# Attention on one core: the order of transposes, copies and small jobs inside a step

## Chip, core and metric

The kernel runs on one core of one Trainium2 chip. The metric is the device time of one execution in microseconds (us), told as the median of several runs. Before the change the median of three runs was 1228.65 us (1227.79 to 1230.59).

## What is computed

The reference is a trunk of two layers on a sequence of 512 tokens with 1024 channels. Layer 0 mixes tokens with a convolution module, layer 1 with a sparse attention; a gated feed-forward stage follows each. The change lies in the attention. With 8 blocks of 64 tokens and 16 blocks to choose from at most, every valid block is selected, and the window of 512 covers the sequence, so both the "selected" and the "window" branch are causal attention over all 512 keys, with keys and values of their own. A third branch attends to 31 compressed blocks. The core of it:

```
def chunk(c):
    ...
    p_c = masked_softmax(s_c, cmp_end[None, :] <= t[:, None])
    o_c = jnp.einsum('bgrqn,bgnd->bgrqd', p_c, v_cmp)
    ...
    p_s = masked_softmax(s_s, tok <= t[:, None])
    o_s = jnp.einsum('bgrqk,bgqkd->bgrqd', p_s, v_s)
    ...
    p_w = masked_softmax(s_w, mask_w)
    o_w = jnp.einsum('bgrqk,bgkd->bgrqd', p_w, vw)
    ...
    return g[0] * o_c + g[1] * o_s + g[2] * o_w
```

There are 16 query heads of 64 channels in 4 groups, and the three outputs are added with a gate for each head and token.

## The kernel before, in words

The whole trunk is one program. The stages follow each other: convolution, first feed-forward, projections of the attention, the loop over heads, the output projection, second feed-forward. Matrix products of the large stages are done in parts: a rounded value and a remainder ("h" and "l" tiles), with three products for one.

The change lies in the loop over heads (the `for n in range(1, N + 2)` at L1861). Its unit of work is a pair of heads, `j` from 0 to 7, and a branch, `br` 1 (selected) or 2 (window), which makes N = 16 units; unit n holds two heads, called `par` 0 and 1 ("head 0" and "head 1" here). A step n does three things at once:

- Scores of unit n: `sc_` calls `score` (L1750) for each of the four query tiles t = 3, 2, 1, 0 of a head. TensorE makes the product S in PSUM (L1760 and L1761, 128 x 128(t+1), at least 256 wide), VectorE (DVE) adds the mask, writes `Pm` to SBUF and takes the extreme value `mx` (L1763), ScalarE (ACT) takes the exponential and its sum `sm` (L1764). Three PSUM banks hold S in turn.
- `weigh_` (L1768): DVE takes the reciprocal of two sums (L1774), and GpSimd (POOL) scales the two tiles by it and by the gate (L1778).
- Unit n - 1, scored and weighed in the step before: `flip_` (L1781) transposes 128 x 128 blocks of `Pm` on TensorE (L1791) into a PSUM bank, four at a time, and one engine copies the bank to SBUF: tag `t1` by DVE (L1794), tags `t0` and `t2` by ACT (L1796). A pair such as (0, 2) means head 0, key block 2; key block kc has 4 - kc transposes, since the mask is causal. So `t2` holds key block 2 of both heads, a `t1` key blocks 1 and 3 of one head, a `t0` key block 0 of one head. `values` (L1800) multiplies them with v (L1817) and adds up in a bank `O`; blocks 3, 2 and 1 at the end of step n, block 0 early in step n + 1.

The transposes, the compressed scores `psc` and the transposed compressed weights `pct` share three PSUM banks (tag "p2"). `O` has two banks of its own.

The compressed branch of a pair of heads is prepared by `q_pair` (L1478). It gives small jobs to named slots "a", "b", "c", "d" of certain steps: `move` (DMAs on the SP queue, L1490), `stack_hi` (L1493, ACT or POOL) and `stack_lo` (L1504, DVE), `scores` (L1509, TensorE, into `psc`), `masked`, `top`, `minus`, `sums` (DVE), `exps` (ACT), `valid` and `weighed` (POOL), `trans` (L1554, four transposes into `pct`) and `parts` (L1560: a rounded copy `pch` by ACT, the remainder `pcl` by DVE). For p = 1, 2, 3 `trans` runs in step 4p, for p = 0 in step 1; `scores` runs in steps 1, 2, 4, 5, 8 and 9. In odd steps `values` begins a new `O` with three products of `pch` and `pcl` (L1809 to L1811). When a head pair is done, in odd steps from 3 on, `o_hi` (ACT, L1828) and `o_lo` (DVE, L1834) copy it out. At the end of steps 14 and 16 a weight of the output projection is split (`w_hi` on ACT, L219; `w_lo` on DVE, L228).

Inside the loop every engine keeps the order in which the program issues its instructions (`tc.keep_in_program_order`); an instruction that waits holds those behind it on its engine. So the order of the calls at L1884 to L1914 is the order of all queues.

Of the kernel before, what the change touches and what calls it, by code (L numbers as in the profile page):

```python
# [120 lines left out]
def trunk(ctx: ExitStack, tc: tile.TileContext, A, out):  # L121
    nc = tc.nc
# [8 lines left out]
    def nm(s):  # L131
        cnt[0] += 1
        return f"{s}_{cnt[0]}"
# [1065 lines left out]
    def nsa(acc, gnext):  # L1199
# [275 lines left out]
        def kept(z):  # L1475
            return tc.keep_in_program_order(z) if fixed[0] else z

        def q_pair(p):  # L1478
# [78 lines left out]
                    tc.keep_in_program_order(nc.tensor.transpose(  # L1557
                        pt[:, t * P:(t + 1) * P], sc[:, t].rearrange("p j n -> p (j n)"), ident))

            def parts():  # L1560
                pt = box["pct"]
                ph = q3[1].tile([P, T], F32R, tag="pch", name=nm("pch"))
                pl = q3[1].tile([P, T], F32R, tag="pcl", name=nm("pcl"))
                kept(nc.scalar.activation(ph, pt, AF.Copy))
                kept(nc.vector.tensor_tensor(pl, pt, ph, ALU.subtract))
                pcT[p] = (ph, pl)

            def both(jj):
# [4 lines left out]
            if p == 0:  # L1573
                return [lambda: (move(0), scores(0), masked(0)), lambda: (both(0), scores(1), masked(1)),
                        lambda: (move(1), top(), minus(), exps()), lambda: (both(1), valid(), sums(), weighed()),
                        trans, parts]
            n = 4 * p - 4
            jobs = {
                (n, "c"): [lambda: scores(0)],
# [19 lines left out]
            }  # L1599
            jobs.update({  # L1600
                (n + 4, "a"): [trans, lambda: stack_hi(1)],
                (n + 4, "c"): [parts],
                (n + 4, "d"): [lambda: stack_lo(1, 0)],
                (n + 5, "a"): [lambda: stack_lo(1, 1)],
            })
# [194 lines left out]
        def values(Us, kcs):  # L1800


            j, br = Us[0]["j"], Us[0]["br"]
            a = j // 4
            if br == 1 and kcs[0] == 3:
                ob[j] = (p2, pO)[j % 2].tile([P, T], F32, tag="O", name=nm("O"), bufs=1)
                ph, pl = pcT[j // 2]
                ch, cl = vcb[a, j % 2]
                pe(nc.tensor.matmul(ob[j], ch, ph, start=True, stop=False))  # L1809
                pe(nc.tensor.matmul(ob[j], ch, pl, start=False, stop=False))  # L1810
                pe(nc.tensor.matmul(ob[j], cl, ph, start=False, stop=False))  # L1811
            o = ob[j]
            for kc in kcs:
                last = br == 2 and kc == 0
                for par in range(2):
                    g = slice((2 * a + par) * DH, (2 * a + par + 1) * DH)
                    pe(nc.tensor.matmul(o[par * 64:par * 64 + 64, P * kc:], vf[br][:, kc, g], Us[par][kc], start=False,  # L1817
                                        stop=last))
                if last:
                    split_o.append(j)  # L1820
# [40 lines left out]
        for n in range(1, N + 2):  # L1861
            S = n < N
            F = n <= N
            if S:
                start(n)

            def sc_(par, *ts):
                if S:
                    for t in ts:
                        score(U[n][par], t)  # L1870

            def weigh_(par, t):
                if S:
                    weigh(U[n][par], t)

            def flip_(tag, eng, *parts):
                if F:
                    flip([(U[n - 1][par], t) for par, t in parts], tag, eng)

            def slot(z):  # L1880
                for f in work.pop((n, z), ()):
                    f()

            sc_(0, 3, 2)  # L1884
            flip_("t2", nc.scalar, (0, 2), (1, 2))
            if n > 1:
                values(U.pop(n - 2), (0,))
            if n == 1:
                qp0[4]()
            slot("a")  # L1890
            weigh_(0, 2)
            sc_(0, 1, 0)
            slot("b")
            o_hi()
            flip_("t1", nc.vector, (0, 1), (0, 3))
            sc_(1, 3)
            weigh_(0, 0)
            flip_("t1", nc.vector, (1, 1), (1, 3))
            sc_(1, 2)
            o_lo()  # L1900
            if n == 1:
                qp0[5]()
            slot("c")
            flip_("t0", nc.scalar, (0, 0))
            sc_(1, 1, 0)
            weigh_(1, 2)
            flip_("t0", nc.scalar, (1, 0))
            slot("d")
            weigh_(1, 0)
            if n in W_AT:  # L1910
                w_hi(state["next"] + W_AT.index(n))
                w_lo(state["next"] + W_AT.index(n))
            if F:
                values(U[n - 1], (3, 2, 1))  # L1914
        assert not work, work
        fixed[0] = hold[0] = False
        sx.close()
# [180 lines left out]
```

## Time and profile before

| what | value |
|---|---|
| median of three runs | 1228.65 us (1227.79 to 1230.59) |
| the profiled execution's own time | 1228.15 us |
| its span, first to last instruction | 1226.3 us |
| PE (TensorE matmul) busy | 1195.1 us, 97% of the span |
| DVE busy | 901.8 us, 74% |
| ACT busy | 603.5 us, 49% |
| POOL busy | 244.4 us, 20% |
| mean granted TensorE clock | 0.997 |
| the attention loop, steps 1 to 16 | from 687.35 to 832.74 us of the span |

PE is the matmul side of TensorE, PEld its weight load, SP the engine that issues most DMAs. A busy PE means that matmuls are under way, not that they run at their peak. A row of the timeline reads: start in us, duration, engine, line, operation, output and inputs with their shapes, how many instructions are merged into the row, and in brackets how long the engine stood idle before it and what released it. The chain of waits is followed back from an end to whatever released each instruction. Names lose their numbers: `T` is the bank of a transpose, `t` its copy in SBUF, `S` a score, `O` an output.

### The profile page before, as it was taken

To read this page: it belongs to the slowest core of one execution; us is meant where nothing else is said; L and a number is where in the kernel's file an instruction comes from. 1 tells how busy PE (TensorE), PEld (TensorE's weight loads), DVE (VectorE), ACT (ScalarE), POOL (GpSimd) and SP (SyncE) were. 2 spreads that over 40 slices of the span, in tenths; PEclk is the share of its full clock that TensorE was granted. 3 is DMA by queue.
4 is the path that set the end of the run, shared out by engine and by line. 5 is a ranking of instruction groups with operands and counts; after the bars stand their busy time and mean duration, and the time that the engine had idled before them with its cause. 6 is when DMAs were issued, how large, how long until landed. Compare 5 with 4: busy or idle time off the path is not lost.

```text
span 1226.3 us, 22079 instructions
## 1 busy us (share of the span) xinstructions
PE 1195.1 (97%) x8519; PEld 1039.0 (85%) x8519; DVE 901.8 (74%) x1722; ACT 603.5 (49%) x1116; POOL 244.4 (20%) x349
## 2 busy tenths in 40 slices
PE   9999999999999999999998899989999999999998
PEld 6788778799999989987677766657878999998998
DVE  6996598877777576865688778764597777776675
ACT  5221464455555444544344677773354555554443
POOL 2021002011111102211333466651000111110120
PEclk9999999999999999999999999999999999999999
DMA  8748628267777667554156011006323877765882
GB/s 308 269 129 300 174 86 240 86 176 184 184 185 179 151 193 162 122 169 112 59 129 175 28 27 32 13 18 172 115 91 110 198 185 182 190 165 123 227 166 91
DMA packets 88378, 181.11 MB, mean 148 GB/s; under 512 B 36816, under 2 KB 38480, under 8 KB 86736
## 3 DMA queue, kind: packets, MB, share of 16 engines
q1 hardware_dynamic: 66816, 109.99, 29.6%
q0 software_dynamic: 21456, 69.71, 25.0%
q8 instruction: 67, 1.10, 0.4%
q14 instruction: 39, 0.32, 0.1%
HBM read 165.60 MB, written 5.80 MB: 140 GB/s over the span
## 4 chain that ended last, share of the span: by engine, by line
PE 80%; DVE 9%; issue 3%; ACT 3%; DMA 2%; SPq 2%; POOL 1%; DVEq 0%; POOLq 0%; ACTq 0%
PE st L915 28%; PE st L1105 10%; PE pp L281 7%; PE pp L279 7%; PE pp L280 7%; PE st L281 2%; PE st L280 2%; PE st L279 2%; PE cpe L540 2%; PE O L1817 2%; PE T L1791 2%; PE pv L1653 2%; DVE wl L228 1%; PE S L1760 1%; DVE Pm L1763 1%
## 5 line engine op out<-in xcount | busy, mean ns | idle before, releaser
L219 ACT ACTIVATE wh<-wr 128x1024 fp32r<-128x1024 f32 (+4 forms) x150 | 152.8, 1019 | 196.0 <-PE pp L280 63.0
L228 DVE TENSOR_TENSOR wl<-wr,wh 128x1024 fp32r<-128x1024 f32 (+4 forms) x150 | 181.4, 1209 | 47.2 <-ACT wh L219 46.8
L915 PE MATMUL st<-bh,sl 128*128 128x256 f32 x680 | 192.6, 283 | 1.1 <-DVE sl L899 1.1
L915 PE MATMUL st<-bh,sh 128*128 128x256 f32 x680 | 192.7, 283 | 0.0
L915 PE MATMUL st<-bl,sh 128*128 128x256 f32 x680 | 192.0, 282 | 0.0
L281 PE MATMUL pp<-hh,wl 128*128 128x512 f32 x400 | 158.1, 398 | 3.9 <-DVE wl L228 3.9
L279 PE MATMUL pp<-hh,wh 128*128 128x512 f32 x400 | 159.6, 401 | 2.2 <-ACT wh L219 2.1
L280 PE MATMUL pp<-hl,wh 128*128 128x512 f32 x400 | 158.7, 398 | 0.1
L915 PEld LDWEIGHTS st<-bh,sl 128*128 128x128 f32 x680 | 130.2, 192 | 1.5 <-DVE sl L899 1.5
L915 PEld LDWEIGHTS st<-bl,sh 128*128 128x128 f32 x680 | 130.6, 192 | 0.1
L915 PEld LDWEIGHTS st<-bh,sh 128*128 128x128 f32 x680 | 130.0, 191 | 0.1
L899 DVE TENSOR_TENSOR sl<-S,sh 128x512 fp32r<-128x512 f32 x136 | 87.9, 688 | 51.9 <-ACT sh L898 51.9
L279 PEld LDWEIGHTS pp<-hh,wh 128*128 128x128 f32 x400 | 75.4, 189 | 23.4 <-ACT wh L219 4.5
L281 PEld LDWEIGHTS pp<-hh,wl 128*128 128x128 f32 x400 | 75.5, 189 | 23.2 <-DVE wl L228 5.9
L1778 POOL TENSOR_SCALAR Pm<-Pm,sm,gates 128x512 f32<-128x512 f32 (+3 forms) x128 | 81.0, 643 | 62.5 <-DVE sm L1774 59.0
L280 PEld LDWEIGHTS pp<-hl,wh 128*128 128x128 f32 x400 | 75.7, 189 | 18.6 <-issue 1.1
L1764 ACT ACTIVATE Pm<-Pm,mx 128x512 f32<-128x512 f32 (+3 forms) x128 | 71.0, 556 | 39.9 <-DVE mx L1763 35.4
L1105 PE MATMUL st<-oz,soh 128*128 128x256 f32 x448 | 79.7, 280 | 0.0
L898 ACT ACTIVATE sh<-S 128x512 fp32r<-128x512 f32 x136 | 77.5, 619 | 0.0
L915 PE MATMUL st<-bl,wh 128*128 128x256 f32 x272 | 76.2, 280 | 0.0
L915 PE MATMUL st<-bh,wh 128*128 128x256 f32 x272 | 76.1, 280 | 0.0
L915 PE MATMUL st<-bh,wl 128*128 128x256 f32 x272 | 76.1, 280 | 0.0
(308 smaller groups left out, 2770.1 us busy)
## 6 DMA issues: line engine op xcount, KB each, us to landing
S<-fw_x POOLq DMA_DIRECT2D x68, 512.0 KB, 5.9
wr<-fw_in SPq DMA_DIRECT2D x46, 512.0 KB
So<-fw_q POOLq DMA_DIRECT2D x38, 448.0 KB, 6.4
bd<-bands POOLq DMA_DIRECT2D x12, 1280.0 KB, 12.4
wr<-fw_q SPq DMA_DIRECT2D x24, 448.0 KB
r<-fw_x SPq DMA_DIRECT2D x34, 256.0 KB
wr<-fw_p SPq DMA_DIRECT2D x16, 512.0 KB
wr<-cw_in SPq DMA_DIRECT2D x14, 512.0 KB
```

Source lines behind the costliest of these rows:

```text
L219: parted(after(nc.scalar.activation(hi[:, :cols], raws[i][:, :cols], AF.Copy), pin.get(AF)))
L228: parted(after(nc.vector.tensor_tensor(lo[:, :cols], raws[i][:, :cols], hi[:, :cols], ALU.subtract), pin.get(ALU)))
L279: held(nc.tensor.matmul(ps, wh, xh, start=first, stop=False))
L280: held(nc.tensor.matmul(ps, wh, xl, start=False, stop=False))
L281: held(nc.tensor.matmul(ps, wl, xh, start=False, stop=last))
L540: last["conv"] = nc.tensor.matmul(ps[e * 64:e * 64 + 16 * m, g, :], w, f[:, g0 + g, 4 - s:68 - s], start=s == 0, stop=s == 4)
L898: pe(nc.scalar.activation(h_[:, c], z, AF.Copy))
L899: pe(nc.vector.tensor_tensor(l_[:, c], z, h_[:, c], ALU.subtract))
L915: pe(nc.tensor.matmul(ps[:, :H], p_[:, k], m_[c][:, t], start=first and c == 0 and q == 0, stop=last and c == 3 and q == 2, skip_group_che ...
L1105: pe(nc.tensor.matmul(ps, a[:, c], b[:, t], start=p in (1, 4) and i == 0 and r == 0, stop=i == NO - 1 and r == 2, skip_group_check=True))
L1764: kept(nc.scalar.activation(Pt, Pt, AF.Exp, bias=mx, scale=-1.0, accum_out=sm))
L1778: kept(nc.gpsimd.tensor_scalar(Pt, Pt, sm[:, k:k + 1], gates[:, t + k, br * 16 + h:br * 16 + h + 1], ALU.mult, ALU.mult))
```

## The change

The transposes and copies of a step come in another order. Before, the order was `t2` of both heads (ACT), `t1` of head 0 (DVE), `t1` of head 1 (DVE), `t0` of head 0 (ACT), `t0` of head 1 (ACT). After, it is `t1` of head 0, `t0` of head 0, `t2` of both heads, `t1` of head 1, `t0` of head 1, on the same engines. `o_hi` moves from behind slot b to behind slot a, `o_lo` from behind the score (1, 2) to ahead of it. The job `parts` is split: `part_hi` (ACT) goes to slot b and `part_lo` (DVE) to slot c, where both were. Slot b now stands behind the `t0` of head 0. In step 1 the jobs of p = 0 go through the slots a, b and c too. The products of `values` at the end of a step take key blocks 2, 3, 1 in place of 3, 2, 1. No instruction is added or taken away.

```
--- before.py
+++ after.py
@@ -1557,12 +1557,15 @@
                     tc.keep_in_program_order(nc.tensor.transpose(
                         pt[:, t * P:(t + 1) * P], sc[:, t].rearrange("p j n -> p (j n)"), ident))
 
-            def parts():
-                pt = box["pct"]
+            def part_hi():
                 ph = q3[1].tile([P, T], F32R, tag="pch", name=nm("pch"))
+                kept(nc.scalar.activation(ph, box["pct"], AF.Copy))
+                pcT[p] = (ph,)
+
+            def part_lo():
+                ph, = pcT[p]
                 pl = q3[1].tile([P, T], F32R, tag="pcl", name=nm("pcl"))
-                kept(nc.scalar.activation(ph, pt, AF.Copy))
-                kept(nc.vector.tensor_tensor(pl, pt, ph, ALU.subtract))
+                kept(nc.vector.tensor_tensor(pl, box["pct"], ph, ALU.subtract))
                 pcT[p] = (ph, pl)
 
             def both(jj):
@@ -1573,7 +1576,7 @@
             if p == 0:
                 return [lambda: (move(0), scores(0), masked(0)), lambda: (both(0), scores(1), masked(1)),
                         lambda: (move(1), top(), minus(), exps()), lambda: (both(1), valid(), sums(), weighed()),
-                        trans, parts]
+                        trans, part_hi, part_lo]
             n = 4 * p - 4
             jobs = {
                 (n, "c"): [lambda: scores(0)],
@@ -1599,7 +1602,8 @@
             }
             jobs.update({
                 (n + 4, "a"): [trans, lambda: stack_hi(1)],
-                (n + 4, "c"): [parts],
+                (n + 4, "b"): [part_hi],
+                (n + 4, "c"): [part_lo],
                 (n + 4, "d"): [lambda: stack_lo(1, 0)],
                 (n + 5, "a"): [lambda: stack_lo(1, 1)],
             })
@@ -1802,7 +1806,7 @@
 
             j, br = Us[0]["j"], Us[0]["br"]
             a = j // 4
-            if br == 1 and kcs[0] == 3:
+            if br == 1 and 3 in kcs:
                 ob[j] = (p2, pO)[j % 2].tile([P, T], F32, tag="O", name=nm("O"), bufs=1)
                 ph, pl = pcT[j // 2]
                 ch, cl = vcb[a, j % 2]
@@ -1881,27 +1885,26 @@
                 for f in work.pop((n, z), ()):
                     f()
 
+            if n == 1:
+                for z, f in zip("abc", qp0[4:]):
+                    work.setdefault((n, z), []).insert(0, f)
             sc_(0, 3, 2)
-            flip_("t2", nc.scalar, (0, 2), (1, 2))
+            flip_("t1", nc.vector, (0, 1), (0, 3))
             if n > 1:
                 values(U.pop(n - 2), (0,))
-            if n == 1:
-                qp0[4]()
             slot("a")
+            o_hi()
             weigh_(0, 2)
             sc_(0, 1, 0)
+            flip_("t0", nc.scalar, (0, 0))
             slot("b")
-            o_hi()
-            flip_("t1", nc.vector, (0, 1), (0, 3))
             sc_(1, 3)
             weigh_(0, 0)
+            flip_("t2", nc.scalar, (0, 2), (1, 2))
+            o_lo()
+            sc_(1, 2)
+            slot("c")
             flip_("t1", nc.vector, (1, 1), (1, 3))
-            sc_(1, 2)
-            o_lo()
-            if n == 1:
-                qp0[5]()
-            slot("c")
-            flip_("t0", nc.scalar, (0, 0))
             sc_(1, 1, 0)
             weigh_(1, 2)
             flip_("t0", nc.scalar, (1, 0))
@@ -1911,7 +1914,7 @@
                 w_hi(state["next"] + W_AT.index(n))
                 w_lo(state["next"] + W_AT.index(n))
             if F:
-                values(U[n - 1], (3, 2, 1))
+                values(U[n - 1], (2, 3, 1))
         assert not work, work
         fixed[0] = hold[0] = False
         sx.close()
```

More of the change, by code (lines that the diff above doesn't have):

```diff
@@ L1558, in trans, with part_hi, part_lo @@
                         pt[:, t * P:(t + 1) * P], sc[:, t].rearrange("p j n -> p (j n)"), ident))
-            def parts():
-                pt = box["pct"]
+            def part_hi():
                 ph = q3[1].tile([P, T], F32R, tag="pch", name=nm("pch"))
+                kept(nc.scalar.activation(ph, box["pct"], AF.Copy))
+                pcT[p] = (ph,)
+            def part_lo():
+                ph, = pcT[p]
                 pl = q3[1].tile([P, T], F32R, tag="pcl", name=nm("pcl"))
-                kept(nc.scalar.activation(ph, pt, AF.Copy))
-                kept(nc.vector.tensor_tensor(pl, pt, ph, ALU.subtract))
+                kept(nc.vector.tensor_tensor(pl, box["pct"], ph, ALU.subtract))
                 pcT[p] = (ph, pl)
@@ L1575, in q_pair @@
                         lambda: (move(1), top(), minus(), exps()), lambda: (both(1), valid(), sums(), weighed()),
-                        trans, parts]
+                        trans, part_hi, part_lo]
             n = 4 * p - 4
@@ L1601, in q_pair @@
                 (n + 4, "a"): [trans, lambda: stack_hi(1)],
-                (n + 4, "c"): [parts],
+                (n + 4, "b"): [part_hi],
+                (n + 4, "c"): [part_lo],
                 (n + 4, "d"): [lambda: stack_lo(1, 0)],
@@ L1804, in values @@
             a = j // 4
-            if br == 1 and kcs[0] == 3:
+            if br == 1 and 3 in kcs:
                 ob[j] = (p2, pO)[j % 2].tile([P, T], F32, tag="O", name=nm("O"), bufs=1)
@@ L1882, in slot @@
                     f()
+            if n == 1:
+                for z, f in zip("abc", qp0[4:]):
+                    work.setdefault((n, z), []).insert(0, f)
             sc_(0, 3, 2)
-            flip_("t2", nc.scalar, (0, 2), (1, 2))
+            flip_("t1", nc.vector, (0, 1), (0, 3))
             if n > 1:
                 values(U.pop(n - 2), (0,))
-            if n == 1:
-                qp0[4]()
             slot("a")
+            o_hi()
             weigh_(0, 2)
             sc_(0, 1, 0)
+            flip_("t0", nc.scalar, (0, 0))
             slot("b")
-            o_hi()
-            flip_("t1", nc.vector, (0, 1), (0, 3))
             sc_(1, 3)
             weigh_(0, 0)
+            flip_("t2", nc.scalar, (0, 2), (1, 2))
+            o_lo()
+            sc_(1, 2)
+            slot("c")
             flip_("t1", nc.vector, (1, 1), (1, 3))
[L1899 to L1904, printed above, removed]
             sc_(1, 1, 0)
@@ L1913, in nsa @@
             if F:
-                values(U[n - 1], (3, 2, 1))
+                values(U[n - 1], (2, 3, 1))
         assert not work, work
```

## The prediction

> **What bounds the kernel now.** I read the page first, then cut its attention loop into its sixteen steps with the table of busy time by stretch, and then went to the chain of waits and the timeline inside single steps. The page's chain of work that ended last gives the first answer:
>
> ```profile
> PE 80%; DVE 9%; issue 3%; ACT 3%; DMA 2%; SPq 2%; POOL 1%; DVEq 0%; POOLq 0%; ACTq 0%
> ```
>
> TensorE (PE) carries four fifths of the end time, so an edit that only reorders work can win no more than the stretches in which PE stands still or runs slowly. The edit lies in the loop of steps n = 1 to 16. I cut it where PE starts the first score of a step. The rows are n = 1, 2, 3, 4, 6, 7, 8, 11, 12, 13, 15 and 16; the columns are the stretch, its length, then PE, PEld, DVE, ACT and POOL busy, the granted TensorE clock and the DMA share:
>
> ```profile
> 687.35:698.39 11.04, 9.12 (x65) 6.90 (x63) 7.21 (x29) 8.33 (x24) 5.15 (x9) 1.00 0.00 0
> 698.39:706.84 8.45, 8.45 (x62) 6.32 (x60) 6.71 (x25) 6.00 (x19) 4.67 (x8) 1.00 0.15 33
> 706.84:715.14 8.30, 8.30 (x57) 5.88 (x55) 7.45 (x26) 6.74 (x22) 6.08 (x10) 1.00 0.15 34
> 715.14:725.50 10.36, 9.22 (x67) 6.79 (x65) 7.63 (x29) 7.78 (x23) 6.79 (x11) 1.00 0.01 2
> 734.64:742.25 7.61, 7.61 (x54) 5.43 (x52) 5.72 (x23) 5.50 (x16) 3.72 (x8) 1.00 0.00 0
> 742.25:751.62 9.37, 8.52 (x57) 5.86 (x55) 8.94 (x28) 8.00 (x26) 7.92 (x11) 1.00 0.27 59
> 751.62:761.98 10.36, 9.22 (x67) 6.80 (x65) 7.59 (x29) 7.65 (x22) 6.67 (x10) 1.00 0.01 2
> 778.73:788.11 9.38, 8.53 (x57) 5.88 (x55) 8.94 (x28) 8.01 (x26) 7.92 (x11) 1.00 0.13 30
> 788.11:796.29 8.18, 8.18 (x59) 5.83 (x57) 5.50 (x21) 6.14 (x17) 5.57 (x9) 1.00 0.00 0
> 796.29:808.07 11.78, 10.33 (x58) 6.61 (x56) 8.04 (x32) 7.84 (x26) 6.44 (x10) 0.86 0.01 3
> 815.67:826.04 10.37, 9.13 (x57) 6.04 (x56) 6.76 (x24) 8.07 (x25) 4.93 (x9) 1.00 0.15 52
> 826.04:832.74 6.70, 6.20 (x42) 3.30 (x40) 2.02 (x4) 3.38 (x7) 4.01 (x8) 1.00 0.49 175
> ```
>
> In n = 6 PE is busy for all of 7.61 us: that is a full step without extras. The other full steps price the extras. A compressed score (`scores`) costs 8.45 - 7.61 = 0.84 (n = 2), the three products with `pcT` that open an odd step's output cost 8.30 - 7.61 = 0.69 (n = 3), the transpose of the compressed weights (`trans`) costs 8.18 - 7.61 = 0.57 (n = 12). With these the losses are: n = 4 and 8, which have `trans` and `scores`, should take 9.02 and lose 1.34 each; n = 7, 11, 13 and 15 should take 8.30 and lose 1.07, 1.08, 3.48 and 2.07; n = 1 and n = 16 have no full twin, and lose at least the time in which PE is not busy, 11.04 - 9.12 = 1.92 and 6.70 - 6.20 = 0.50. That is 12.8 us in all, and the change can reach no more. What PE waits for in this loop, in the table of waits (total, times, longest):
>
> ```profile
> PE T L1791 <- ACT t L1796: 4.0, 4, 1.1
> PE T L1791 <- POOL Pm L1778: 3.6, 4, 1.5
> ```
>
> Two kinds of wait, both ahead of a transpose. One is for a PSUM bank that an ACT copy still reads, the other for POOL, which has not yet scaled the weights of head 1.
>
> **The wait for POOL (n = 7, 11, 13, 16).** The chain at the start of n = 7:
>
> ```profile
> 742.22 2.15 POOL Pm L1778 x2
> 744.37 0.04 issue
> 744.41 0.44 PE T L1791 x2
> ```
>
> The old step opens with the t2 transposes, and two of their four blocks are head 1's (1,2), which POOL scales late in the step before (742.22 to 744.37, while n = 7 begins at 742.25). The new step opens with head 0's t1 blocks, scaled before them on POOL's queue, and asks for (1,2) only in the fourth group, in place of the old second t1 group. By n = 6 that is about 3.9 us after the step's start (the fourth group, one before the one at 739.37 below), here 746.2, nearly 2 us after POOL is done. So this wait goes whole: 1.07 + 1.08 in n = 7 and 11, 0.4 of the 0.50 in n = 16 (I keep 0.1 for the last head 1 copy there, which now has less in front of it). What is late next is that copy, `t0` of head 1 on ACT, before value product 0 of the next step; it keeps its place and its follower.
>
> In n = 13 the same wait is followed by a slow stretch:
>
> ```profile
> 796.30:799.70 3.40, 1.95 (x12) 1.15 (x12) 3.32 (x13) 2.38 (x9) 2.32 (x3) 1.00 0.01 2
> 799.70:803.20 3.50, 3.50 (x13) 1.90 (x13) 0.97 (x6) 1.50 (x5) 2.33 (x4) 0.51 0.02 5
> 818.00:821.00 3.00, 2.02 (x14) 1.54 (x13) 2.05 (x5) 1.39 (x5) 0.00 (x0) 1.00 0.28 79
> ```
>
> PE stood for 1.45 of 3.40 us, and for the next 3.50 us the clock was 0.51; with 0.98 of 3.00 us idle (n = 15) it stayed at 1.00. Half speed for 3.4 us costs 3.4 x 0.5 = 1.70 of the 3.48. I take it that the stop brought the slow stretch, so both go: 3.48.
> The Trainium skill, "TensorE: Matmul & The Clock Gate", Part 1, says the clock drops after at least one idle window of about 3.4 us. The trace differs as far as 1.45 us of idleness came before the drop; by the rule this stop is too short to cause it, and 1.70 us less would be won (first rival).
>
> **The wait for the bank (n = 1, 4, 8).** The end of the old n = 4, from the same chain:
>
> ```profile
> 722.38 0.48 ACT pch L1564
> 722.87 0.49 ACT t L1796
> 723.36 0.14 issue
> 723.50 0.63 PE T L1791 x4
> ```
>
> Three banks serve all transposes. Late in n = 4 the transposed weights `pct` hold one until `pcl` is out, a score `psc` holds one, and the last transposes stand behind one ACT copy that queues behind `pch`. The change splits the job: `pch` in slot b, behind the new early t0 copy, `pcl` in slot c. To see when it comes I lay the ACT queue of n = 6 out anew:
>
> ```profile
> 737.58 0.57 ACT L1796 ACTIVATE t<-T 128x512 f32<-128x512 f32 x1
> 738.05 0.62 ACT L1501 ACTIVATE St<-q 128x512 fp32r<-128x512 f32 x1
> 738.57 0.49 ACT L1764 ACTIVATE Pm<-Pm,mx 128x256 f32<-128x256 f32 x1
> ...
> 739.07 0.39 ACT L1764 ACTIVATE Pm<-Pm,mx 128x128 f32<-128x128 f32 x1
> ...
> 739.65 0.73 ACT L1764 ACTIVATE Pm<-Pm,mx 128x512 f32<-128x512 f32 x1
> ```
>
> The t2 copy leaves 737.58, so the cast of `St` takes its place and the exponentials of (0,1) can start at about 738.2, when DVE has the maximum (its reciprocal is at 737.70, below). From start to start they take 0.50 and 0.39, the t0 copy 0.47, the exponential of (1,3) 0.73, the t2 copy 0.57: the t0 copy ends near 739.6 (4.9 after the step's start), the t2 copy near 740.87 (6.2 after). In n = 4 `trans` puts all that 0.57 later, so `pch` runs from about 5.5 to 6.0 and DVE's `pcl`, behind the maximum of (1,2), ends near 6.6. PE in n = 6:
>
> ```profile
> 739.37 0.60 PE L1791 MATMUL T<-cc,Pm 128*128 128x128 f32 x4
> ...
> 740.28 0.60 PE L1791 MATMUL T<-cc,Pm 128*128 128x128 f32 x4
> 740.81 1.52 PE L1817 MATMUL O<-t,v 128*64 128x128 f32 x12
> ```
>
> The group at 739.37 is 4.7 into the step; `trans` and `scores` move it to 6.1 in n = 4. It gets a free bank at 6.6 if it is given that of `pct`, a loss of 0.5; given that of t2 (6.2 + 0.57 + 0.48 for `pch` = 7.3) it loses 1.1. I take 0.5, since `pct` is free first: 1.34 - 0.5 = 0.84 each for n = 4 and 8, ends 0.2 and 0.9. In n = 12 there is no score to cover it: the value products, 6.2 + 0.57 = 6.7 into the step, meet the t2 copy at 7.3, so a new loss of 0.55 (0.3 to 1.1). In n = 1 there is no value product 0, PE runs ahead and ACT and DVE are the limit; I take 0.8 of the 1.92 (0 to 1.9).
>
> **The order 2, 3, 1 and the t2 copy.** In n = 6 the products start at 740.81 with block 2, whose copy I put at 740.87: with the wake-up 0.1 lost in each of n = 6, 10 and 14 (0 to 0.3 each). Odd steps have 0.69 and steps with a score 0.84 of cover. Block 3 and 1 of head 1 need the DVE copy that the change puts behind the maximum of (1,2); it has the time of the last transposes and of block 2.
>
> **DVE's new second copy.** The t1 copy now stands ahead of the reciprocal of (0,2), which waits for ACT anyway; a copy takes 682 ns on average and fits into the 1.00 us:
>
> ```profile
> L1794 DVE COPY t<-T 128x512 f32<-128x512 f32 x32 | 21.7, 682 | 3.2 <-PE T L1791 3.1
> ```
> ```profile
> 737.70 0.17 DVE L1774 RECIPROCAL sm<-sm 128x2 f32<-128x2 f32 x1 [1.00 <-ACT Pm L1764]
> ```
>
> Were its transposes late, the reciprocal, POOL's scaling and the next maxima would queue behind it; its blocks are the oldest that POOL has, so I cost it at nothing.
>
> **n = 15.** Here the weight split of the next stage holds DVE, first on ACT, then itself:
>
> ```profile
> 816.66 1.05 ACT L219 ACTIVATE wh<-wr 128x1024 fp32r<-128x1024 f32 x1
> ```
> ```profile
> 817.74 1.22 DVE L228 TENSOR_TENSOR wl<-wr,wh 128x1024 fp32r<-128x1024 f32 x1 [1.26 <-ACT wh L219]
> ```
>
> A copy less stands between the last exponentials and this cast, so it comes 0.47 earlier, and the DVE copy placed into the reciprocal's wait gives some 0.3 more: 0.8 of the 2.07 (0 to 1.2).
>
> **Moved at no cost.** `o_hi` takes the hole on ACT that the t2 copy leaves in odd steps, `o_lo` stays behind head 0's reciprocal. The moves issued by SP and the weight loads keep their order on SP's queue, and POOL's queue keeps its order, since no slot passes another.
>
> **Sum.** 0.8 (n = 1) + 2 x 0.84 (4, 8) + 1.07 + 1.08 (7, 11) + 3.48 (13) + 0.8 (15) + 0.4 (16) - 0.55 (12) - 0.3 (6, 10, 14) = 8.46 us. The profiled execution took 1228.15, its span 1226.3; the median of the runs is 1228.65, 0.50 above it. So 1219.7 for a like execution and 1220.2 for the median. With the better ends (1.9, 2 x 0.9, 1.07, 1.08, 3.48, 1.2, 0.5, less 0.3) the gain is 10.7: 1217.9.
>
> **The rivals.**
> - *The slow clock stays, or comes elsewhere.* The half clock is not the stop's work, or new stops in n = 1 bring one. For it: one case only links stop and slow stretch. Against: the milder stop in n = 15 had none after it. Gain 8.46 - 1.70 = 6.76: 1221.9. Chance 0.20. By the Trainium skill's rule on idle windows, weighed above, it would be this one.
> - *The waits only change their names.* The banks are handed out the worse way and ACT stays the limit: nothing won in n = 1, 4, 8 and 15, 1.1 lost in n = 12, 0.3 in each of 6, 10, 14. Left: 1.07 + 1.08 + 3.48 + 0.4 - 1.1 - 0.9 = 4.03: 1224.6. Chance 0.13. With the first rival on top 2.33: 1226.3.
> - *Slower: block 2 waits for ACT in every step.* The t2 copy has moved from the front of ACT's step to its middle, and its product from second to first. If ACT reaches it 1.4 us later than I laid out, n = 6, 10, 12, 14 lose about 1.5 each, the five odd steps without a score 0.8, the five steps from n = 2 on with one 0.6: 13.0 lost against 8.46 won, 1233.2. It decides from about 1.0 us. For it: my margin in n = 6 is nil. Against: ACT has the room, 5.50 of 7.61 us busy. Chance 0.08.
> - *No change.* The loop ends earlier, but the stage after it waits for its weights as long. For it: the last step's DMA share is already 0.49. Against: that is prefetch issued in the loop's own order, which moves with it. 1228.65. Chance 0.09.
>
> **How the numbers follow.** The forecast has 0.50. A measurement of this kernel tells about 0.2%, 2.5 us, from no change. Faster by more: 0.50 + 0.20 + 0.13 = 0.83; within: 0.09; slower: 0.08. The range takes in the better ends (1217.9) and the first two rivals together (1226.3), and leaves out the 0.17 of the last two.
>
> **What would show it.** Right: no PE transpose waits for POOL in the loop; n = 7 and 11 take about 8.3 us, n = 4 and 8 about 9.5, n = 13 about 8.3 with the clock at 1.00, n = 12 about 8.7. Wrong: PE products behind ACT's t2 copy in most steps, a 0.5 clock row inside the loop, or n = 4 and 8 still above 10 us.

## The result and the profile after

The changed kernel took 1222.55 us (median of four runs, 1220.94 to 1224.96), the kernel before beside it 1229.1 (four runs, 1227.79 to 1230.59). The ratio is 0.9948, with a 95% interval of 0.9927 to 0.9969: by the ratio 6.4 us less, and the interval holds 3.8 to 9.0. Timed again beside the experiments below, the kernel before had medians of 1228.09 (31 runs), 1226.61 (15) and 1226.22 (11), so the gain may well lie in the lower half of that interval. The profiled execution of after took 1224.96 us, the slowest of its four, with a span of 1223.2 and a mean clock of 1.000.

The summary line of the chain on the page of after:

```profile
PE 80%; DVE 9%; DMA 3%; ACT 3%; issue 2%; SPq 2%; POOL 1%; DVEq 0%; POOLq 0%; ACTq 0%
```

It differs from that of before only in "issue", 2% for 3%. Nothing can be learned about an edit inside 145 us from shares of 1223. The table of busy time by stretch shows it. The loop of after, cut where the prediction cut it; the rows are n = 1, 2, 3, 4, 6, 7, 8, 11, 12, 13, 15 and 16, the columns the stretch, its length, then PE, PEld, DVE, ACT and POOL busy, the granted clock and the DMA share:

```profile
689.60:700.00 10.40, 9.19 (x66) 7.00 (x64) 7.39 (x29) 8.00 (x24) 4.83 (x9) 1.00 0.00 0
700.00:708.74 8.74, 8.65 (x62) 6.34 (x60) 6.81 (x25) 6.21 (x20) 4.89 (x8) 1.00 0.14 32
708.74:717.96 9.22, 8.55 (x57) 5.93 (x55) 7.54 (x26) 6.74 (x22) 6.16 (x10) 1.00 0.14 30
717.96:727.56 9.60, 9.29 (x67) 6.74 (x65) 7.49 (x28) 7.24 (x22) 6.46 (x11) 1.00 0.01 2
...
736.71:744.48 7.77, 7.67 (x54) 5.49 (x53) 6.01 (x23) 5.93 (x18) 4.16 (x8) 1.00 0.01 2
744.48:753.85 9.37, 8.74 (x58) 5.92 (x56) 9.04 (x28) 7.48 (x24) 7.14 (x10) 1.00 0.26 58
753.85:763.44 9.59, 9.28 (x66) 6.73 (x64) 7.48 (x28) 7.23 (x22) 6.45 (x11) 1.00 0.01 3
...
780.37:789.73 9.36, 8.76 (x58) 5.94 (x56) 9.03 (x28) 7.48 (x24) 7.12 (x10) 1.00 0.14 30
789.73:798.41 8.68, 8.37 (x59) 5.77 (x57) 7.38 (x28) 7.14 (x22) 6.42 (x11) 1.00 0.00 0
798.41:806.71 8.30, 8.30 (x58) 5.88 (x56) 6.24 (x25) 6.79 (x21) 5.41 (x10) 1.00 0.01 4
...
814.48:824.07 9.59, 9.02 (x57) 6.00 (x55) 6.92 (x25) 7.61 (x22) 5.96 (x9) 1.00 0.19 56
824.07:830.03 5.96, 5.96 (x42) 3.32 (x40) 2.04 (x4) 3.01 (x5) 3.33 (x7) 1.00 0.43 159
```

Set against the rows of before, step for step (minus is shorter):

| n | 1 | 2 | 3 | 4 | 6 | 7 | 8 | 11 | 12 | 13 | 15 | 16 |
|---|---|---|---|---|---|---|---|---|---|---|---|---|
| after - before, us | -0.64 | +0.29 | +0.92 | -0.76 | +0.16 | 0.00 | -0.77 | -0.02 | +0.50 | -3.48 | -0.78 | -0.74 |

With n = 10 and 14 (+0.17 each) and 5 and 9 (+0.01) the loop goes from 145.39 to 140.43 us, 4.96 less. The spans differ by 3.1: after's loop began at 689.60 where before's began at 687.35, 2.25 later, and what follows it took 0.39 less. The change does not touch what lies ahead of the loop; three profiles of one and the same kernel (below) began it at 687.2, 688.3 and 691.2. A single span therefore cannot tell this change to better than some 4 us, while the lengths of the steps can.

The waits of after, PE's lines of the table (total, times, longest):

```profile
PE S L1764 <- DVE mx L1767: 1.5, 3, 0.6
PE psc L1513 <- ACT t L1800: 0.9, 1, 0.9
PE T L1795 <- ACT t L1800: 0.9, 2, 0.7
PE T L1795 <- DVE pcl L1568: 0.6, 3, 0.2
```

The 3.6 us behind POOL are gone, and 4.0 behind ACT's copies became 0.9 + 0.9. In their place PE's scores wait for DVE's maximum (before: 1.0, once). Lines from 1568 on stand 3 or 4 lines further down than in before: L1795 is the transpose, L1800 the ACT copy, L1798 the DVE copy, L1767 the maximum, L1782 POOL's scaling.

### The profile page after: what moved, and what is told of

It reads as the page before. It is cut to its first block, busy times and chain, and to the rows that moved or that the text cites. A ratio compares the mean times of both kernels' runs of the same rounds, so it can differ in the third digit from the quotient of the medians.

```text
span 1223.2 us, 22084 instructions
## 1 busy us (share of the span) xinstructions
PE 1193.2 (98%) x8519; PEld 1037.3 (85%) x8519; DVE 901.7 (74%) x1722; ACT 601.7 (49%) x1116; POOL 246.5 (20%) x349
## 4 chain that ended last, share of the span: by engine, by line
PE 80%; DVE 9%; DMA 3%; ACT 3%; issue 2%; SPq 2%; POOL 1%; DVEq 0%; POOLq 0%; ACTq 0%
PE st L915 28%; PE st L1105 10%; PE pp L281 7%; PE pp L279 7%; PE pp L280 7%; PE O L1821 3%; PE st L281 2%; PE st L280 2%; PE st L279 2%; PE cpe L540 2%; PE T L1795 2%; PE pv L1657 2%; DVE wl L228 1%; PE S L1764 1%; PE S L1765 1%
## 5 line engine op out<-in xcount | busy, mean ns | idle before, releaser
L228 DVE TENSOR_TENSOR wl<-wr,wh 128x1024 fp32r<-128x1024 f32 (+4 forms) x150 | 180.0, 1200 | 46.6 <-ACT wh L219 46.2
L1782 POOL TENSOR_SCALAR Pm<-Pm,sm,gates 128x512 f32<-128x512 f32 (+3 forms) x128 | 81.6, 648 | 58.3 <-DVE sm L1778 51.2
```

The source lines that it names most:

```text
L228: parted(after(nc.vector.tensor_tensor(lo[:, :cols], raws[i][:, :cols], hi[:, :cols], ALU.subtract), pin.get(ALU)))
L1782: kept(nc.gpsimd.tensor_scalar(Pt, Pt, sm[:, k:k + 1], gates[:, t + k, br * 16 + h:br * 16 + h + 1], ALU.mult, ALU.mult))
```

## The experiments

For each kernel the loop was cut into steps, from the first weight load of a step to that of the next (in n = 1 that is 0.12 us ahead of PE's first score, from which the rows above count). At full clock, two traces with the same order agree step by step within 0.02 us, so lengths of steps are compared across kernels; the total times are given beside them. Each ratio is to the kernel before, timed beside that run. The edits are written out plainly and shortened to the lines that matter (`...` marks lines left out); the kernels that ran make the same choices by constants.

| kernel | loop, us | n=1 | 3 | 4 | 7 | 12 | 13 | 15 | 16 |
|---|---|---|---|---|---|---|---|---|---|
| before | 145.51 | 11.16 | 8.30 | 10.36 | 9.37 | 8.18 | 11.78 | 10.37 | 6.70 |
| before, second profile | 143.90 | 11.17 | 8.30 | 10.35 | 9.38 | 8.17 | 10.18 | 10.37 | 6.70 |
| after | 140.55 | 10.52 | 9.22 | 9.60 | 9.37 | 8.68 | 8.30 | 9.59 | 5.96 |
| order only | 144.77 | 11.39 | 9.22 | 10.57 | 9.37 | 10.08 | 8.30 | 9.59 | 5.96 |
| split only | 139.25 | 10.06 | 8.30 | 9.25 | 9.38 | 8.18 | 8.82 | 10.36 | 6.71 |
| new order in step 13 only | 142.74 | 11.15 | 8.30 | 10.35 | 9.38 | 8.17 | 9.02 | 10.36 | 6.71 |

**Order only.** The new order of transposes and products, with `parts` in one place again (rounded copy and remainder both in slot c):

```
--- after
+++ order only
-                (n + 4, "b"): [part_hi],
-                (n + 4, "c"): [part_lo],
+                (n + 4, "c"): [part_hi, part_lo],
...
-                for z, f in zip("abc", qp0[4:]):
+                for z, f in reversed(list(zip("acc", qp0[4:]))):
```

> The kernel after, but the two halves of the job parts stay together in slot c; the rest of the change stands. Theory (the split frees the bank of the transposed weights early): the rounded copy pch goes back behind the exponential of (1,2) on ACT, so steps 4 and 8 take 10.2 to 10.8 us in place of the 9.6 of the kernel after, step 12 about 9.3 in place of 8.68, and the loop is 1.5 to 3 us longer than the kernel after's 140.43. Rival (the new order of the transposes alone is what counts): steps 4, 8 and 12 stay within 0.2 us of the kernel after.

Measured: 1227.33 us, ratio to before 0.9999 [0.9981, 1.0016]: no change. Without the split, n = 4 and 8 are longer than before, as expected, and n = 12 loses 1.9, more than expected. The end of n = 4 in the timeline of this kernel:

```profile
729.08 0.58 ACT L1562 ACTIVATE pch<-pct 128x512 fp32r<-128x512 f32 x1
729.69 0.69 DVE L1568 TENSOR_TENSOR pcl<-pct,pch 128x512 fp32r<-128x512 f32 x1 [1.86 <-ACT pch L1562]
730.50 0.42 PEld L1795 LDWEIGHTS T<-cc,Pm 128*128 128x128 f32 x4 [0.88 <-issue]
730.53 0.63 PE L1795 MATMUL T<-cc,Pm 128*128 128x128 f32 x4 [0.70 <-DVE pcl L1568]
```

DVE stands 1.86 us for `pch`, and the last transposes stand behind `pcl` for the bank. Over the loop the order alone wins nothing (144.77, against 143.90 of before at full clock). It wins 1.5 in n = 15 and 16 and loses 2.4 in the other steps. Its 8.30 in n = 13 is paid for in n = 12: the two together take 18.38, and 18.35 in the second profile of before.

**Split only.** The old order and the old order of products, with `part_hi` in slot b and `part_lo` in slot c.

```
--- before
+++ split only
-                (n + 4, "c"): [parts],
+                (n + 4, "b"): [part_hi],
+                (n + 4, "c"): [part_lo],
...
+            if n == 1:
+                for z, f in zip("abc", qp0[4:]):
+                    work.setdefault((n, z), []).insert(0, f)
...
```

> The kernel before, with the job parts split over slots b and c and nothing else of the change. Theory (split and order each remove a wait of their own): steps 4 and 8 fall from 10.36 to about 9.2 us, since pch no longer queues late on ACT; step 13 keeps its wait for POOL and its slow clock, 11 us or more; the loop is about 3 us shorter than before's 145.39. Rival (the late pcl on DVE in step 12 is what made POOL late in step 13): step 13 falls to 8.3 to 9 us too, the clock stays at 1.00, and the loop is 6 to 7 us shorter than before, shorter than that of the kernel after, because steps 2, 3, 6, 10, 12 and 14 do not get longer.

Measured: 1222.74 us, ratio 0.9954 [0.9932, 0.9976], the same gain as the whole change. The loop is 1.3 us shorter than after's. All of n = 1, 4 and 8 is there (1.1 each), and step 13 falls to 8.82 with the *old* order, as the rival in the expectation had it. How a job in step 12 shortens step 13 is seen on three queues. Before, step 12 begins at 788.11 and 13 at 796.29:

```profile
795.25 0.57 ACT L1564 ACTIVATE pch<-pct 128x512 fp32r<-128x512 f32 x1
795.86 0.69 DVE L1565 TENSOR_TENSOR pcl<-pct,pch 128x512 fp32r<-128x512 f32 x1 [1.25 <-ACT pch L1564]
797.02 0.16 DVE L1774 RECIPROCAL sm<-sm 128x2 f32<-128x2 f32 x1
797.38 2.83 POOL L1778 TENSOR_SCALAR Pm<-Pm,sm,gates 128x512 f32<-128x512 f32 x3 [2.75 <-DVE sm L1774]
```

Split only, step 12 begins at 789.30 and 13 at 797.48:

```profile
794.06 0.58 ACT L1562 ACTIVATE pch<-pct 128x512 fp32r<-128x512 f32 x1
795.72 0.69 DVE L1568 TENSOR_TENSOR pcl<-pct,pch 128x512 fp32r<-128x512 f32 x1
796.87 0.16 DVE L1778 RECIPROCAL sm<-sm 128x2 f32<-128x2 f32 x1
797.20 3.23 POOL L1782 TENSOR_SCALAR Pm<-Pm,sm,gates 128x512 f32<-128x512 f32 x4 [1.38 <-DVE sm L1778]
799.09 0.44 PE L1795 MATMUL T<-cc,Pm 128*128 128x128 f32 x2 [0.30 <-POOL Pm L1782]
```

Counted from the start of step 12, `pch` starts at 7.14 before and at 4.76 here; DVE's wait of 1.25 is gone; the reciprocal comes at 8.91 and at 7.57; POOL begins 1.09 after step 13's start and 0.28 ahead of it. These 1.37 us are the 1.36 by which step 13 is shorter (10.18, without the slow clock, to 8.82). Most of the wait "for POOL" that the prediction read in n = 13 was a late `pch` on ACT, two engines up the chain. For n = 7 and 11 this does not hold: no `pch` stands in the step before them.

**New order in step 13 only.** The kernel before, with the new order in n = 13 alone (products 3, 2, 1, no split).

```
--- before
+++ new order in step 13 only
-            flip_("t2", nc.scalar, (0, 2), (1, 2))
+            if n == 13:
+                flip_("t1", nc.vector, (0, 1), (0, 3))
+            else:
+                flip_("t2", nc.scalar, (0, 2), (1, 2))
...
+            if n == 13:
+                flip_("t0", nc.scalar, (0, 0))
...
```

> The kernel before, with the new order of transposes, copies, o_hi and o_lo in step 13 alone. Theory (the stop for POOL brings the slow clock): step 13 falls from 11.78 to about 8.3 us and no stretch of the loop runs at half clock; every other step keeps its length; the gain is 3.5 us. Rival (the slow clock comes of its own): step 13 takes about 10.0 us and a stretch of 3.4 us at a granted clock near 0.5 stays in the loop; the gain is 1.8 us.

Measured: 1225.66 us, ratio 0.9985 [0.9970, 1.0000]; step 13 is 9.02, the others as before. That is 0.72 more than expected, though no transpose waits for POOL in it any more; what holds the rest was not tested. So in this one step the order is worth 10.18 - 9.02 = 1.16 and the split 1.36. Either does more than half of it, both together 1.88 (8.30).

**The kernel before, profiled again, twice.** This asks whether the half clock in step 13 belongs to the stall.

> The kernel before, unchanged, profiled once more. It asks whether the half clock in step 13 belongs to the stall of 1.45 us there or to where that stall falls on the chip's own clock of windows. Theory (chance of position): all steps repeat to within 0.02 us of the first profile, and step 13 is either 11.78 again with a row of half clock near 800 us, or, if the stall falls otherwise in its window, 11.78 - 1.70 = 10.08 with the clock at 1.00. Rival (the stall always brings it): 11.78 with the half clock, whatever the start of the loop. 11.78 leaves both standing; 10.08 refutes the rival.

> The kernel before once more, a third profile of step 13, with the same two theories: 10.08 at full clock, or 11.78 with 3.4 us at half clock. The loop sums to 145.4 us with the half clock and to 143.7 without.

Measured: 1227.43 and 1230.3 us; step 13 took 10.18 and 10.17. The first of them, the first two stretches of step 13:

```profile
797.38:800.70 3.32, 1.85 (x10) 1.05 (x8) 3.25 (x13) 2.31 (x9) 2.23 (x3) 1.00 0.01 2
800.70:804.20 3.50, 3.50 (x24) 2.52 (x23) 2.25 (x10) 2.55 (x9) 2.44 (x4) 1.00 0.02 5
```
```profile
800.34 0.44 PE L1791 MATMUL T<-cc,Pm 128*128 128x128 f32 x2 [1.47 <-POOL Pm L1778]
```

The same stall, 1.47 us (1.45 in the first profile), is followed by a full clock, where the first profile had 0.51 for 3.50 us. All other steps agree within 0.02.

Does it matter where the stall falls? In each trace the slow stretches start on one grid of 3.413 us: in the first profile at 612.03, 799.76 and 1226.42, which are 55 and 125 windows apart. In the first profile the stall (797.79 to 799.24) lies inside one window of the grid, 796.35 to 799.76. In the second (798.87 to 800.34) it straddles two, with the edge at 799.80, which would explain the full clock. But in the third (801.76 to 803.22) it lies inside one again, with PE busy for 1.95 of 3.41 us where the first profile had 1.96, and the clock of the next window is 1.00:

```profile
800.95:804.36 3.41, 1.95 (x11) 0.93 (x10) 2.87 (x11) 3.00 (x10) 3.01 (x4) 1.00 0.01 2
804.36:807.78 3.42, 3.42 (x27) 3.02 (x26) 2.64 (x11) 2.36 (x7) 2.15 (x4) 1.00 0.02 5
```

So neither the stall nor PE's busy time in its window decides alone, and what does stays open. The third profile, at 1230.3, is the slowest of the three and has its half clock ahead of the loop. So 11.78 - 10.18 = 1.60 of step 13's 3.48 is not a fixed part of the kernel before.
The Trainium skill, "TensorE: Matmul & The Clock Gate", Part 1, says that the clock is judged in a free-running window of 3413 ns, so that the point of change depends on where in the window the work falls. The traces agree on the window: slow stretches of 3.41 us or twice that, on one grid. That the place in the window decides is not borne out by the third profile. The page's rule of a whole idle window before the drop does not fit the 1.45 us of idleness in 3.40.

**Old order of products.** The whole change, with `values` taking 3, 2, 1 again.

```
--- after
+++ old order of products
-                values(U[n - 1], (2, 3, 1))
+                values(U[n - 1], (3, 2, 1))
```

> The kernel after, but the products at the end of a step in the old order 3, 2, 1. Theory (the order 2, 3, 1 matters because the copy of head 1's t1 blocks is now the later one): in step 6 that copy ends 0.5 us after the products start, so steps without a score (6, 10, 12, 14) take 0.2 to 0.5 us more than in the kernel after and the loop 1 to 3 us more. Rival (the t2 copy on ACT is the later one, so the old order would be the better): these steps take 0.1 to 0.2 us less, 7.6 in place of 7.77.

Measured: 1223.92 us, ratio 0.9976 [0.9957, 0.9996]. The loop is 140.87, 0.32 longer than after's; n = 6 and 10 lose 0.41 each and n = 7 and 11 win 0.39 each, 14 wins 0.16 and 15 loses 0.19 (what one step yields the next takes), 16 loses 0.25. The order 2, 3, 1 is worth 0.3 us, nearly all of it in the last step. The expectation had 1 to 3 us, and named the right steps only for 6 and 10.

**Split, with the new order in 7 and 11 only.** Products in the order 3, 2, 1.

```
--- split only
+++ split, new order in 7 and 11
-            flip_("t2", nc.scalar, (0, 2), (1, 2))
+            if n in (7, 11):
+                flip_("t1", nc.vector, (0, 1), (0, 3))
+            else:
+                flip_("t2", nc.scalar, (0, 2), (1, 2))
...
```

> The split of parts as in the kernel before with the split alone, and the new order of transposes and copies in steps 7 and 11 only. Theory (in steps 6 and 7 DVE is the limit: its chain runs without a hole through two stack_lo slowed to 1.15 and 1.51 us beside POOL): the wait for POOL goes but steps 7 and 11 keep 9.2 to 9.4 us. Rival (the prediction's step: POOL alone holds the start of these steps): they fall to 8.3 to 8.5 us, since step 6 stays in the old order.

Measured in one run: 1222.51 us; n = 7 and 11 take 9.65 and 9.64, 0.27 *longer* than with the old order. There the new order loses outright, although no transpose waits for POOL.

**Mask job left out.** The whole change, without `valid` for head pairs 2 and 3. This kernel leaves the compressed weights of these pairs unmasked.

```
--- after
+++ mask job left out
-                (n + 3, "a"): [valid, lambda: stack_lo(0, 1)],
+                (n + 3, "a"): [lambda: stack_lo(0, 1)],
```

> The kernel after without the job valid for the head pairs 2 and 3: their compressed weights are not multiplied by the table of valid blocks, so POOL has 1.3 us less in steps 7 and 11. Theory (POOL's valid slows the stack_lo of step 7 on DVE from about 0.7 to 1.51 us, and DVE's maximum behind it holds PE): that stack_lo falls to 0.7 to 1.0 us and steps 7 and 11 take 8.6 to 8.9 in place of 9.37. Rival (POOL's scaling slows it as much, or the work ahead on DVE is what counts): the stack_lo stays above 1.1 us and the steps above 9.1.

Measured in one run: 1220.62 us; n = 7 and 11 take 8.53, 0.84 less than in after, all other steps as there. What stands in the way in after, the timeline of n = 7:

```profile
746.98 0.69 DVE L1798 COPY t<-T 128x512 f32<-128x512 f32 x1
...
747.27 1.28 POOL L1537 TENSOR_TENSOR sc<-sc,cc 128x512 f32<-128x512 f32 x1
...
747.59 1.51 DVE L1507 TENSOR_TENSOR St<-q,St 64x512 fp32r<-64x512 f32 x1
...
749.03 0.15 DVE L1778 RECIPROCAL sm<-sm 128x2 f32<-128x2 f32 x1
...
749.56 0.44 PE L1764 MATMUL S<-kst,St 128*128 128x384 f32 x1 [0.56 <-DVE mx L1767]
```

The same place without `valid`:

```profile
744.86 0.67 DVE L1507 TENSOR_TENSOR St<-q,St 64x512 fp32r<-64x512 f32 x1
745.45 0.15 DVE L1778 RECIPROCAL sm<-sm 128x2 f32<-128x2 f32 x1
```

And before, where `stack_lo` (L1507) began first:

```profile
745.01 0.85 DVE L1507 TENSOR_TENSOR St<-q,St 64x512 fp32r<-64x512 f32 x1
...
745.29 1.72 POOL L1537 TENSOR_TENSOR sc<-sc,cc 128x512 f32<-128x512 f32 x1
```

In after POOL's mask starts 0.32 us ahead of DVE's `stack_lo`, takes 1.28, and `stack_lo` takes 1.51: until POOL's end at 748.55, and then 0.55 more. Before, DVE began 0.28 ahead, and POOL paid with 1.72 for 1.28. What let POOL in is the t1 copy, which the change has put ahead of `stack_lo` on DVE: in its place, at 746.98, `stack_lo` would have begun 0.29 ahead of the mask (an estimate from these rows). From the start of `stack_lo` to the reciprocal it takes 1.44 in after and 0.59 without the mask, and the difference of 0.85 is the 0.84 of the step. With the old order in the steps around it (the run above) the same two instructions took 1.28 and 1.51 again.
The Trainium skill, "SBUF — State Buffer", section "Who interferes with whom", says that a DVE instruction with two SBUF inputs and a GpSimd instruction that reads SBUF hold one port pair in turn, and that whichever comes second blocks. The trace agrees, with 1.51 against 0.67 for one order and 1.72 against 1.28 for the other.

**Early maxima.** The whole change, with `top` and `minus` of the compressed scores moved forward to the end of steps 2, 5 and 9; `exps` follows in slot a of step 3 and slot b of steps 6 and 10.

```
--- after
+++ early maxima
-                (n + 1, "d"): [lambda: masked(1), lambda: move(0)],
+                (n + 1, "d"): [lambda: masked(1), lambda: move(0), top, minus],
...
-                (n + 2, "c"): [top],
-                (n + 2, "d"): [minus, exps, lambda: stack_lo(0, 0)],
+                (n + 2, "b"): [exps],
+                (n + 2, "d"): [lambda: stack_lo(0, 0)],
...
-                (2, "d"): [lambda: masked(1), lambda: stack_lo(0, 1)],
-                (3, "a"): [top, minus, exps],
+                (2, "d"): [lambda: masked(1), lambda: stack_lo(0, 1), top, minus],
+                (3, "a"): [exps],
```

> The kernel after with the jobs top and minus one step earlier, at the end of steps 2, 5 and 9, and exps following in step 3 slot a and steps 6 and 10 slot b. Theory (top and minus behind the new DVE copy hold ACT's exps and all behind it in step 3, and fill DVE in steps 6, 7, 10 and 11): step 3 falls from 9.22 to 8.3 to 8.5, steps 7 and 11 from 9.37 to 8.3 to 8.8, steps 2, 5 and 9 grow by 0.3 at most; the loop takes about 137.5 us in place of 140.5. Rival (the extra time of step 3 comes from the order of the copies itself): step 3 stays above 9 us and the time moves elsewhere.

Measured: 1222.38 us, ratio 0.9968 [0.9952, 0.9984]. n = 3 falls from 9.22 to 8.42, n = 7 and 11 from 9.37 to 8.81; n = 6 and 10 rise from 7.77 to 8.26, so each of these pairs gives back 0.49 of 0.56. `stack_lo` still takes 1.60 in n = 7 there. The loop is 141.16, about 139.6 with after's n = 1 in place of the one below, for an expected 137.5. What n = 3 lost in after is named by this run. Its chain in after, in order of time:

```profile
710.70 0.60 DVE t L1798
711.30 0.60 DVE cm L1528
711.90 0.02 issue
711.92 0.70 DVE sc L1531
712.63 0.02 issue
712.65 0.63 ACT sc L1534
...
714.64 0.49 ACT t L1800
715.13 0.14 issue
715.26 0.63 PE T L1795 x4
```

The t1 copy stands ahead of `top` (L1528) and `minus` (L1531) on DVE; `exps` (L1534) starts 0.6 later and holds ACT's queue; behind it, the exponentials and the t0 copy come late, and the last transposes wait for that bank. With `top` and `minus` gone from there, all but 0.12 of the loss goes.
One step of this run can't be compared: n = 1 took 12.06 with a slow stretch of 3.40 us in it, where the same order took 10.52 in after. So a slow stretch can come in the loop with the new order too.

**Combination.** The split, the early maxima, the old order and products 3, 2, 1 in steps 1 to 12, the new order of transposes from 13 on.

```
--- early maxima
+++ combination
-            flip_("t1", nc.vector, (0, 1), (0, 3))
+            if n > 12:
+                flip_("t1", nc.vector, (0, 1), (0, 3))
+            else:
+                flip_("t2", nc.scalar, (0, 2), (1, 2))
...
-                values(U[n - 1], (2, 3, 1))
+                values(U[n - 1], (3, 2, 1))
```

> The split of parts, the early top and minus, the old order of transposes and products in steps 1 to 12, the new order of transposes from step 13 on. Theory (the split wins most of the gain, the new order pays only in steps 13, 15 and 16, the early top frees steps 7 and 11): steps 4 and 8 about 9.25, steps 7 and 11 8.3 to 8.6, step 13 8.3, step 15 9.6, step 16 6.0, no half clock in the loop; the loop takes about 135.5 us, 10 us less than before's 145.5, and the time is about 10 us below the kernel before's. Rival (the pieces do not add): a step of the list misses its figure by over 0.5 us and the loop stays above 137.

Measured: 1217.8 us (five runs, 1216.78 to 1220.08), ratio 0.9928 [0.9914, 0.9943], so some 8.8 us below the before timed beside it (1226.61), where the change won 6.4. The two intervals overlap, but the loop is 136.73 for after's 140.55 (135.5 was expected: n = 7 and 11 take 8.78, n = 15 9.79). `stack_lo` never takes over 0.70 us there.

**Combination, trimmed.** The same, with the maxima of the second head pair left in step 3 and products 2, 3, 1 in steps 15 and 16.

```
--- combination
+++ combination, trimmed
-                (2, "d"): [lambda: masked(1), lambda: stack_lo(0, 1), top, minus],
-                (3, "a"): [exps],
+                (2, "d"): [lambda: masked(1), lambda: stack_lo(0, 1)],
+                (3, "a"): [top, minus, exps],
...
-                values(U[n - 1], (3, 2, 1))
+                values(U[n - 1], (2, 3, 1) if n > 14 else (3, 2, 1))
```

> The version with the split, the old order up to step 12 and the new one from 13, with two steps mended: the maxima of the compressed scores of the second head pair stay in step 3 (their early place had cost there: step 3 8.61 against 8.30), and the products of steps 15 and 16 come in the order 2, 3, 1 (9.79 and 6.21 against 9.59 and 5.96 in the changed kernel). Theory (the lengths of steps add up, since each is set by its own order): step 3 8.30, step 15 9.59, step 16 5.96, all others as in the version before it, the loop 136.73 - 0.31 - 0.20 - 0.25 = 135.97; the median 0.76 below, about 1217.0. Rival (what one step wins its neighbour gives back): the loop stays at 136.5 or above, with step 4 or 14 longer by what steps 3 and 15 win.

Measured: 1217.15 us (seven runs, 1216.27 to 1223.47), ratio 0.9929 [0.9915, 0.9944]. The steps n = 15 and 16 in the table of busy time by stretch:

```profile
812.70:822.47 9.77, 9.04 (x57) 6.00 (x56) 6.93 (x25) 7.79 (x24) 6.16 (x9) 1.00 0.15 55
822.47:828.42 5.95, 5.95 (x42) 3.32 (x40) 2.03 (x4) 3.01 (x5) 3.45 (x8) 1.00 0.47 168
```

Steps 3 and 16 came as expected (8.30 and 5.95), step 15 did not: 9.77, not 9.59. In after step 14, with 2, 3, 1, is 0.17 longer (7.77 for 7.60) and 15 is 0.18 shorter: the two belong together. The loop is 136.16 for an expected 135.97. Its time can't be told from that of the version before it.

## Why the prediction was right, and where its steps were not

The time came within the range: 1222.55 for a forecast of 1220.2. Of the 8.46 us that the sum promised, the loop of the profile shows 4.96, and 3.35 when before's loop is taken at full clock. That the time came so near is in part luck, as the paragraph on n = 13 shows. The terms beside what they measured:

| step | forecast gain, us | profile, us |
|---|---|---|
| n = 1 | 0.8 | 0.64 |
| 4 and 8 | 0.84 each | 0.76, 0.77 |
| 7 and 11 | 1.07, 1.08 | 0.00, 0.02 |
| 13 | 3.48 | 3.48, of which 1.60 is the clock |
| 15 | 0.8 | 0.78 |
| 16 | 0.4 | 0.74 |
| 12 | -0.55 | -0.50 |
| 6, 10, 14 | -0.1 each | -0.16, -0.17, -0.17 |
| 3, 2 | 0 | -0.92, -0.29 |

**Right, and shown.** The bank wait of n = 1, 4 and 8 goes through the split, and only through it (split only: 1.1 each; order only: -0.2 each). In after's n = 4 the transposes of head 1's t1 blocks wait 0.19 for `pcl` and start 6.68 us into the step, on the bank on which the prediction bet (it had 6.6). The small losses of n = 6, 10 and 14 came nearly as priced: in n = 6 the weight load of the first product waits 0.33 for the t2 copy. n = 15 and 16 are the order's work: the split alone leaves them at 10.36 and 6.71. In n = 15 DVE's part of the weight split (L228) starts 1.44 us into the step in place of 2.07, 0.63 earlier where 0.47 was forecast. Of the 0.74 of n = 16, 0.25 is the order of the products, which the prediction had not counted there.

**n = 12 had the right size for another reason.** The prediction let the products wait for the t2 copy. In after:

```profile
795.20 0.63 PE L1795 MATMUL T<-cc,Pm 128*128 128x128 f32 x4 [0.20 <-ACT t L1800]
...
795.57 0.69 DVE L1568 TENSOR_TENSOR pcl<-pct,pch 128x512 fp32r<-128x512 f32 x1
...
796.14 0.59 ACT L1800 ACTIVATE t<-T 128x512 f32<-128x512 f32 x1
...
796.41 0.63 PE L1795 MATMUL T<-cc,Pm 128*128 128x128 f32 x4
...
796.96 1.52 PE L1821 MATMUL O<-t,v 128*64 128x256 f32 x12
```

The t2 copy (796.14) is done at 796.73, before the products start at 796.96, right behind the last transposes. It is the transposes that are late: one group stands 0.20 for the bank of the t0 copy. The last group can only have the bank of `pct`, since the copies from the other two run until 796.73 and 796.85, and it starts 0.15 after `pcl`, as in n = 4. So 0.55 for 0.50 was a hit by luck.

**"So this wait goes whole" (n = 7 and 11) failed.** The wait for POOL went, and nothing was won. The prediction asked what is late next on ACT and did not follow DVE: in the rows of before it is busy for 8.94 of 9.37 and 9.38 us, more than PE's 8.52 and 8.53, as in no other step. In after the chain follows it from 740.95 to 749.50 without a hole of over 0.04 us, and the step has 9.04 us of work for it; its `stack_lo` is drawn out to 1.51 us by POOL's mask, and PE waits for the maximum behind it. Leaving out the mask gives 0.84 of the 1.07 back.

**"Fits into the 1.00 us wait ... I cost it at nothing" (DVE's new second copy) failed in n = 3.** The hole was read in n = 6, where no small job of DVE stands in slot a. In n = 3, `top`, `minus` and, through them, ACT's `exps` stand there, and a copy of 0.6 us in front of a chain that crosses to ACT cost 0.92. The same holds for n = 7, where `stack_lo` stands in that slot. The prediction named who would queue behind a *late* copy, not those who queue behind one in time. What n = 2 loses (0.29) was not tested alone: it comes with the order (order only has it, split only does not).

**n = 13 was right in size for mixed reasons.** The prediction gave the whole wait to the order of the transposes. The new order in this step alone wins 1.16, the split alone 1.36, both 1.88. Taken with n = 12, the new order adds nothing to the split: 12 and 13 take 16.98 in after and 17.00 with the split alone, for 18.35 before. And it took the half clock to be the stop's work: two further profiles of the same kernel with the same stop have none. In the profile of before the 1.60 was there to be won; in the median of its runs an unknown part is. That is the rival "the slow clock stays" with another outcome: the clock did not stay, but its loss was not constant either, and the run with early maxima had it in n = 1. The loop of before without it, 143.9, less that of after, 140.55, is 3.35 us, a little under the 3.8 at the lower end of the interval; with it 4.96, inside. How often the timed runs had a slow stretch there is not known. But the mean clock of most executions is on record, and 1.000 leaves no room for a stretch of 3.41 us (one such stretch makes 0.999). Twelve later executions of before at 1.000 have a median of 1225.4, the three of after at 1.000 have 1221.8. That is 3.6 us, close to the loop's 3.35. So some 3 us of the 6.4 are likely slow stretches and scatter in the four runs of before, which the sum did not forecast.

**The rivals.** The waits did change names in part (POOL to DVE in n = 7 and 11), not in the way that rival laid out: n = 1, 4, 8 and 15 won. The slower case did not come: n = 6, 10 and 14 lost 0.17, not 1.5. The loop won 3.50 us less than the sum; 2.13 of it are n = 7 and 11, 1.21 are n = 2 and 3, and the rest of the terms differ by 0.16 in all. But for n = 2 this is one cause, the DVE copy put forward.

Seen by parts, against a loop of 143.9: the split wins 4.65 alone; the two new orders lose 0.87 alone and 1.30 on top of the split, since they win 2.04 in n = 13, 15 and 16 and lose 3.3 in the other steps.

## What to carry to other kernels

A wait names the engine that came last, not the one that was late: follow the queue of the releaser back until an engine had something to do the whole time, here, in n = 13, from POOL over DVE's reciprocal to one ACT copy. When an instruction is put forward on an engine, price it in every step by what stands behind it there, not in the step where a hole was seen; an order that pays in some steps can be kept for those alone, which here, with the split kept and the early maxima added, gave a loop of 136.16 us for 140.55. A step that has the forecast length can have it for another reason, and one step's gain can be its neighbour's loss: check the wait, and add up neighbours. Where a program runs in repeating steps, compare step lengths over traces: they settle tenths of a microsecond where total times scatter by several.

## What the runs showed of the hardware

- At full clock, step lengths repeat within 0.02 us from trace to trace, while the start of the loop moved from 686.5 to 692.6 us of the span over thirteen traces, all of kernels that are the same up to there.
- One program with the same stall (1.45 and 1.47 us) ran the 3.4 us after it at a clock of 0.51 in one trace and at 1.00 in two others. The slow stretches of a trace last 3.41 or 6.83 us and start on one grid of 3.413 us (first profile of before: 612.03, 799.76, 1226.42). PE busy for 1.96 of a window of the grid was followed by a half clock, 1.95 of one by a full clock.
- A DVE subtraction of two SBUF operands of 64 x 512 took 0.67 us, and 1.51 when a POOL instruction on SBUF had begun 0.32 us earlier; in the other order POOL took 1.72 in place of 1.28, and DVE 0.85.
